# A fused SSD and attention layer on one core: the softmax division moved behind the value product, and the last norm part put into the issue table

## The chip, the cores and the metric

The kernel runs on one core of a Trainium2 chip. The time is device microseconds of one execution. Before the change three runs gave 640.44, 639.76 and 640.36 us, median 640.36.

## The reference

One layer of a streaming encoder, in fp32, for 512 tokens of a new stream ("prompt") and 64 tokens of a running one ("sample") with 256 cached frames. D = 1024. Cut to what the change touches:

```python
def mla_attend(...):
    s = einsum(q_lat, keys_c) + einsum(q_rope, keys_r)
    s = jnp.where(mask, s * scale, -jnp.inf)
    pr = jax.nn.softmax(s, axis=-1)          # the division by the row sum
    return einsum('bhqk,bkl->bqhl', pr, keys_c)
...
x = x + concat([y_ssd, o]) @ w_out
hf = rmsnorm(x, norm_ffn)
x = x + (silu(hf @ w_gate) * (hf @ w_up)) @ w_down
y = rmsnorm(x, norm_final)
```

There are eight attention heads of 64 value columns. The softmax divides each row of exponentials by its sum; the value product then sums over keys. The final norm divides every token by the root of its mean square over the 1024 channels. Beside this the layer has a chunked SSD (Mamba-2) branch with a causal convolution, whose output `y_ssd` is the other half of the input of `w_out`.

## The kernel before

Activations lie with channels on the 128 partitions and the 576 tokens (512 + 64) along the free axis. Most fp32 products are made of three fp32r products: each operand is split into a high part (ACT cast, L127/L157/L719) and a low part (DVE subtract, L128/L159/L720), so an evacuation of a product that feeds another product costs one ACT and one DVE instruction.

The stages by the trace: first projections and convolution until about 90 us, the SSD until about 150, attention with the output product until about 235, the gate/up and down products (Strassen-like block products, L894, L1034) until about 601, and last the final down tiles with the final norm (L1132 to L1262) until the end.

Attention works on pairs of heads `p` = 0..3. For a pair and a block of 128 query tokens `i` = 0..3, `scores` (L680) makes one PSUM bank `sc` per head, up to 512 keys wide; `soft` (L656 to L671) takes the row maximum on DVE (`mx`, L663), the exponential on ACT with the row sum accumulated (`pr`, `sm`, L664), the reciprocal of both sums on DVE (L665), and divides: head 0 by a DVE multiplication (L670), head 1 by an ACT scaling (L668). `turn` (L702, L704) transposes the divided blocks on PE into banks `ptp` of the tag "pp" and copies them to SBUF as `pt`, head 0 by ACT, head 1 by DVE. `values` (L727) sums V times `pt` into a bank `pv`, also of tag "pp", 64 partitions per head and 512 tokens wide; `cat` (L719, L720) splits `pv` into high and low parts `cat_o`. `out_tile` multiplies with `w_out` (banks `ps_o`); its first half takes `cat_y` (the SSD output), its second half `cat_o` of the four pairs. The sample tokens (`i` = 4, banks `sc_s`, `ptp_s`, `pvs`) go the same way with 64 tokens.

The last stage computes the eight channel tiles of y in two column parts of 320 and 256 tokens. For part 1 (256 columns) each tile t has 12 matmuls into `ps_l1_t` (L1104), a DVE addition to the residual `x2[t]` (L1145), an ACT square (`sq`, L1233) and, for t < 7, an ACT scaling with the gain (L1149). Squares of tiles 0 to 3 are summed by POOL, and ones-matmuls (`packed`, L1203) sum over channels. Ln and Exp on ACT and three DVE instructions make the norm factor (L186 to L193), eight small matmuls spread it over the partitions (`ps_r`, L1257), ACT copies one of the two spread banks to SBUF (`R`, L1258), and the tiles are multiplied by it: t = 0 and 1 on POOL from `R` (L1157), the others on DVE from PSUM (L1159, L1155), then stored.

Inside each engine the order of instructions is not left to a scheduler: a table of ranges per engine (`ISSUE`) lists the program's instructions in the order in which the engine issues them, and a second table (`PLACES`) says which buffer slot each tile gets. SP issues nearly all weight loads in one such order. Only the last part of the final norm stood outside of the table, in a block with a manual schedule (L1210 onward), in program order.

Of the kernel before, what the change touches and what calls it, by code (L numbers as in the profile page):

```python
# [19 lines left out]
P = 128  # L20
# [17 lines left out]
BLOCKS = tuple(range(0, LAST - 1, 4))  # L38
SEEDED = (4, 5, 6, 7)
# [17 lines left out]
def hybrid_layer_kernel(ctx: ExitStack, tc: tile.TileContext, a, o):  # L57
# [596 lines left out]
    prs, pts = {}, {}  # L654

    def soft(p, i, scs, nk):  # L656

        n = len(scs)
        mx = ap_.tile([P, 2], F32, tag="mx", name="mx", bufs=4)
        sm = ap_.tile([P, 2], F32, tag="sm", name="sm", bufs=4)  # L660
# [4 lines left out]
        dve.reciprocal(sm[:, :n], sm[:, :n])  # L665
        for j in range(n):
            if j:
                act.activation(pr[:, j], pr[:, j], AF.Identity, scale=sm[:, j : j + 1])  # L668
            else:
                dve.tensor_scalar(pr[:, j], pr[:, j], sm[:, j : j + 1], None, ALU.mult)  # L670
        prs[p, i] = pr  # L671

# [49 lines left out]
    def values(p):  # L722
        pv = bank("pp", f"pv{p}")
        for b in range(4):
            for j in range(2):
                h = 2 * p + j
                pe.matmul(  # L727
                    pv[64 * j : 64 * j + 64, b * P :], V[b][:, h * HD : (h + 1) * HD], pts[p, b, j],
                    start=b == 0, stop=True, skip_group_check=b > 0,
                )  # L730
        cat(p, pv, slice(0, TP))
# [464 lines left out]

    W1 = parts[1].stop - parts[1].start
# [11 lines left out]
    with tc.manual_schedule(engines={pe.engine, dve.engine, pool.engine, act.engine}):  # L1209
        pn0, pn1 = lbank("sc", "ps_n3_0", 0), bank("pp", "ps_n3_1")  # L1210
        first, second, _ = norm_steps(pn0, pn0, D, eps=False)
        q = []
        sent = [set(), set()]

        def out(i, k, r, rp):
            t = ORDERS[i][k]
            outs(i, t, r, rp)
            sent[i].add(t)
            if i == 0 and t ^ 1 in sent[i]:
                send(i, t & 6, 2, sp)  # L1220

        for t in range(KT):
            p = lbank(("hm", "sc", "pp")[t % 3], f"ps_l1_{t}", 1)
            down_half(p, last_terms(t), parts[1])
            if t == 2:
                pe.matmul(pn0, ones, ss3[:, parts[0]], start=True, stop=True)
                first()
            add(t, 1, p)
            if t == 2:
                second()  # L1230
                act.copy(R3[:, parts[0]], pn0)
            q.append(tmp("sq", W1))
            act.activation(q[t], x2[t][:, parts[1]], AF.Square)  # L1233
            if t < KT - 1:
                gain(t, 1)

            for k in {0: (), 1: (1, 0)}.get(t, (t,) if t < NP else ()):
                pool.tensor_tensor(ss3[:, parts[1]], ss3[:, parts[1]], q[k], ALU.add)  # L1238
            for k in OUTS.get(t, ()):
                out(0, k, pn0, R3[:, parts[0]])  # L1240
        packed(pn1, ss3[:, parts[1]], True, False)
        for t in range(NP, KT):
            packed(pn1, q[t], False, t == KT - 1)
        Rp = tmp("Rp", W2)
        first, second, _ = norm_steps(Rp, pn1[:, :W2], D, eps=False)
        first()
        second()

        warm = bank("hm", "ps_warm_last")
        for _ in range(7):  # L1250
            pe.matmul(warm[:, :P], ones, ones, start=True, stop=True)

        pr1 = [lbank("sc", f"ps_r3_{z}", 1) for z in range(2)]
        for z in pr1:
            for hf in range(2):
                row = ident[:, 64 * hf : 64 * hf + 1].to_broadcast([P, P])
                pe.matmul(z[:, hf * W2 : (hf + 1) * W2], row, Rp, start=True, stop=True)  # L1257
        act.copy(R3[:, parts[1]], pr1[1])  # L1258
        for k in range(KT):
            out(1, k, pr1[0], R3[:, parts[1]])  # L1260
        for t, q in SENDS:
            send(1, t, 1, q)  # L1262
# [25 lines left out]
0651423651426340315406516235041350264531645302406124531260546312045123450612345014652051342603541350124365310462054260  # L1288
534132025104623562453163052412365401546210503421602541356041536510223405632140562056143241564032
# [12 lines left out]
021021202120120120120120120120120102102012102102102102121021021201201201201201210210210202102102021  # L1302
# [3 lines left out]
0120210  # L1306
# [12 lines left out]
142-147 152-171 174 270-271 175-177 272-274 178-187 172-173 188-269 275-370 373-420 371 421-468 372 469-601 613-636  # L1319
602-612 637 641-644 638-640 657-659 665-688 660 689-736 661-662 737-760 771-794 663-664 645-652 763-766 653-656  # L1320
795-818 767-770 761-762 819-826 859-861 833-836 862-864 827-832 865-866 837-839 867 880-883 840 868-870 841 845-852
871-873 853-856 874-879 842-843 904-906 857-858 884-887 907-909 844 888 910-912 892-903 889-891 913-915 925-934
916-921 935 939-940 922-924 936-938 949-957 964-965 941 966 945-948 967-969 942-944 970-971 958-963 972-974 976-979
975 987-988 980 984-985 1003 991-993 981-983 986 1015 1004-1006 989 994-995 1016-1021 996 1007-1014 1022-1026
1029-1034 997 1043-1045 990 1000-1002 998-999 1046-1054 1035-1042 1027-1028 1059-1060 1055 1075-1092 1056-1058
1093-1104 1121-1123 1065-1067 1124 1061-1062 1071-1072 1063-1064 1130-1132 1068-1070 1125-1129 1073 1133-1156
1105-1108 1074 1229-1237 1119-1120 1238 1241 1239-1240 1242-1252 1157 1111-1114 1109-1110 1253-1264 1158 1176
1265-1276 1115-1118 1159-1161 1177-1179 1162-1175 1277-1285 1289-1290 1180-1183 1188-1189 1184-1187 1205-1206
1190-1192 1227 1193-1198 1291-1297 1199-1201 1228 1202-1204 1286-1288 1215-1220 1207-1214 1221 1318 1222-1224 1298
1225-1226 1299-1306 1319 1307 1320 1308-1317 1321-1322 1330-1332 1323 1342-1343 1348-1351 1344-1345 1352-1354 1346  # L1330
1355 1347 1333 1324-1329 1334-1341 1356-1363 1368 1364-1366 1369-1370 1367 1371-1393 1404 1394-1396 1405-1406
1397-1403 1407-1415 1428 1416-1427 1429-1433 1440-1441 1434-1435 1442 1436-1439 1572 1443-1447 1452 1448 1453-1456
1449 1457-1458 1450 1459-1460 1451 1461-1462 1587 1578 1584 1463 1581 1573 1464-1478 1579 1479-1486 1575 1488 1487
1489 1585 1490-1497 1500 1498 1501-1503 1499 1586 1588 1504-1506 1576 1574 1507 1580 1508-1509 1512 1577 1513 1510
1514-1515 1511 1516-1517 1605 1518-1522 1593 1523-1525 1582-1583 1526-1527 1606 1528-1531 1602 1536 1532 1537 1533
1538 1534 1603 1539 1607 1535 1589 1540-1541 1599 1542-1544 1594 1608 1545-1550 1600 1551-1552 1595 1614 1553-1555
1609 1560 1556-1557 1626 1561-1565 1615 1558-1559 1566-1568 1616 1569-1570 1604 1571 1596 1590 1597-1598 1601 1591
1610 1617 1620 1623 1621 1635 1627 1622 1592 1636 1629 1637 1628 1611 1641 1618 1630 1624 1631 1612-1613 1625
1658-1659 1642 1644 1650 1660 1647 1661-1662 1632-1633 1663 1651 1648 1664-1665 1619 1656 1638-1640 1666 1643 1667
1634 1668 1645 1669 1646 1649 1652-1654 1657 1694 1670-1672 1695-1697 1673 1682 1698 1655 1674 1699 1675 1700 1718  # L1340
1683 1719 1676-1677 1701 1678 1684 1702 1679 1685 1703 1680 1704 1686 1681 1720 1687 1721 1688 1722-1723 1689 1724
1690-1691 1706 1692-1693 1725 1707 1726 1705 1727-1728 1708-1709 1730 1710-1711 1729 1712 1731-1732 1713-1717
1733-1734 1778-1779 1735 1780 1754 1736 1755 1742 1756 1743-1744 1781 1737 1782 1745-1746 1766 1747-1749 1767 1783
1750-1752 1738 1768 1753 1757-1758 1769 1739-1740 1759 1741 1770 1784 1760 1785-1786 1771 1787 1761-1762 1802 1788
1803 1772 1789 1763 1773 1804-1805 1774 1806-1813 1764-1765 1775-1776 1838 1777 1839-1841 1862-1864 1842 1865
# [267 lines left out]
```

## Time and profile before

| what | value |
|---|---|
| median of three runs | 640.36 us |
| the profiled execution's own time | 639.58 us |
| its span (first to last instruction) | 637.5 us |
| around the span | 2.08 us |
| PE busy | 626.2 us, 98% |
| DVE busy | 551.4 us, 86% |
| ACT busy | 390.4 us, 61% |
| POOL busy | 70.7 us, 11% |
| mean granted PE clock | 0.998 |

PE is TensorE's matmul row, PEld its weight loads, DVE VectorE, ACT ScalarE, POOL GpSimd, SP SyncE (which issues DMAs). In a timeline a row is: start, busy time, engine, line, operation, tiles out<-in, shape, count; in brackets the idle time of the engine ahead of it and what ended that. In the table of windows each engine has its busy time in the stretch.

### The profile page before, as it was taken

The numbers are of one execution on the slowest core, as the hardware profiler recorded it, in microseconds if no ns is written. First come the engines' busy times: TensorE is split into PE (matmuls) and PEld (weight loads), VectorE is DVE, ScalarE is ACT, GpSimd is POOL, SyncE is SP. The second block draws the span as 40 slices with busy tenths as digits, with TensorE's granted clock in tenths as the row PEclk, the third lists the DMA queues.
The fourth block names the chain that finished last, engine by engine and source line by source line (L and its number), as shares of the span: only waits on it lengthen the run. The fifth ranks groups of instructions, "written<-read, shape, count | busy, mean of one in ns | idle before, by whom it ended". The sixth has DMA issues, their size and how long they took to land.

```text
span 637.5 us, 11950 instructions
## 1 busy us (share of the span) xinstructions
PE 626.2 (98%) x4639; PEld 598.0 (94%) x4639; DVE 551.4 (86%) x980; ACT 390.4 (61%) x751; POOL 70.7 (11%) x111
## 2 busy tenths in 40 slices
PE   9999999999999999999999999999999999999994
PEld 9899999985887899999999999999999999999994
DVE  6999996899867599999998997889888998998763
ACT  7655425789766479955656565655565656545463
POOL 1322122001010000000012002100211011100022
PEclk9999999999999999999999999999999999999999
DMA  9522185314131132231187427550765274723004
GB/s 310 207 51 78 35 209 151 114 30 147 72 111 34 62 131 73 93 108 67 36 202 158 128 91 163 141 136 40 189 159 133 67 182 111 181 74 133 1 1 149
DMA packets 31560, 72.66 MB, mean 114 GB/s; under 512 B 3706, under 2 KB 11400, under 8 KB 31248
## 3 DMA queue, kind: packets, MB, share of 16 engines
q1 hardware_dynamic: 25360, 60.77, 29.8%
q0 software_dynamic: 5424, 10.57, 9.3%
q8 instruction: 36, 0.59, 0.4%
q10 hardware_dynamic: 720, 0.57, 0.3%
q14 instruction: 20, 0.16, 0.1%
HBM read 58.03 MB, written 3.30 MB: 96 GB/s over the span
## 4 chain that ended last, share of the span: by engine, by line
PE 48%; issue 1%; DVE 1%; ACT 1%; POOL 1%; POOLq 0%; DVEq 0%
PE ps_x L894 17%; PE ps_dx L1034 9%; PE ps_z L894 9%; PE ps_dz L1034 5%; PE ps_y L894 4%; PE ps_dy L1034 2%; PE ps_l L1104 2%; POOL x L1157 0%; DVE x L1145 0%; DVE sq_last L1194 0%; DVE ss L1192 0%; POOL ss L1238 0%; POOLq L1600 0%; ACT sq L1233 0%; ACT x L1149 0%
## 5 line engine op out<-in xcount | busy, mean ns | idle before, releaser
L894 PE MATMUL ps_x<-xop,wh_gu_S 128*128 128x288 f32 x504 | 126.2, 295 | 0.0
L894 PEld LDWEIGHTS ps_x<-xop,wh_gu_S 128*128 128x128 f32 x504 | 88.2, 188 | 0.7 <-ACT u L963 0.2
L894 PE MATMUL ps_x<-xop,wl_gu_S 128*128 128x288 f32 x252 | 73.2, 295 | 0.0
L894 PE MATMUL ps_z<-xop,gu_a 128*128 128x288 f32 x252 | 61.7, 295 | 0.0
L127 ACT CAST wh_gu_S<-gu 128x1024 fp32r<-128x1024 f32 x44 | 46.2, 1053 | 14.8 <-PE ps_y L894 4.2
L128 DVE TENSOR_TENSOR wl_gu_S<-gu,wh_gu_S 128x1024 fp32r<-128x1024 f32 x44 | 52.8, 1217 | 0.8 <-ACT wh_gu_S L127 0.5
L894 PEld LDWEIGHTS ps_x<-xop,wl_gu_S 128*128 128x128 f32 x252 | 47.1, 188 | 0.0
L1047 POOL DMA_DIRECT2D x<-db x16 | 14.9, 930 | 277.9 <-ACT db L1040 247.8
L143 PE MATMUL ps_in<-xs,wh_in 128*128 128x288 f32 x256 | 45.5, 298 | 0.0
L894 PE MATMUL ps_y<-xop,wh_gu_A 128*128 128x288 f32 x168 | 44.9, 295 | 0.0
L894 PEld LDWEIGHTS ps_z<-xop,gu_a 128*128 128x128 f32 x252 | 43.5, 188 | 0.0
L894 PE MATMUL ps_z<-xop,wh_gu_S 128*128 128x288 f32 x168 | 43.4, 295 | 0.0
L894 PE MATMUL ps_x<-xop,wh_gu_A 128*128 128x288 f32 x168 | 42.7, 295 | 0.0
L143 PEld LDWEIGHTS ps_in<-xs,wh_in 128*128 128x128 f32 x256 | 37.8, 189 | 0.2
L127 ACT CAST wh_gu_A<-gu 128x1024 fp32r<-128x1024 f32 x22 | 23.1, 1051 | 23.0 <-PE ps_x L894 16.1
L894 PEld LDWEIGHTS ps_y<-xop,wh_gu_A 128*128 128x128 f32 x168 | 30.1, 188 | 0.1
L894 PEld LDWEIGHTS ps_z<-xop,wh_gu_S 128*128 128x128 f32 x168 | 29.7, 188 | 0.0
L128 DVE TENSOR_TENSOR wl_gu_A<-gu,wh_gu_A 128x1024 fp32r<-128x1024 f32 x22 | 26.8, 1217 | 3.3 <-ACT wh_gu_A L127 1.8
L894 PEld LDWEIGHTS ps_x<-xop,wh_gu_A 128*128 128x128 f32 x168 | 29.5, 188 | 0.0
L465 PE MATMUL ps_o<-cat_y,wh_out 128*128 128x288 f32 x128 | 29.0, 312 | 0.0
L143 PE MATMUL ps_in<-xs,wl_in 128*128 128x288 f32 x128 | 27.5, 296 | 0.0
L465 PE MATMUL ps_o<-cat_o,wh_out 128*128 128x288 f32 x128 | 27.3, 297 | 0.0
(594 smaller groups left out, 2002.8 us busy)
## 6 DMA issues: line engine op xcount, KB each, us to landing
gu<-in_w_gu SPq DMA_DIRECT2D x44, 512.0 KB, 4.8
db<-in_w_down SPq DMA_DIRECT2D x16, 512.0 KB, 4.5
x<-db POOLq DMA_DIRECT2D x16, 288.0 KB, 6.5
x<-dc POOLq DMA_DIRECT2D x16, 288.0 KB, 4.1
wr_in<-in_w_in SPq DMA_DIRECT2D x8, 512.0 KB, 6.2
wr_out<-in_w_out SPq DMA_DIRECT2D x8, 512.0 KB, 3.3
cumb<-cumD SPq DMA_DIRECT2D x5, 512.0 KB, 5.0
x<-in_xT SPq DMA_DIRECT2D x2, 1152.0 KB, 6.6
```

The costliest lines, as they stand in the source:

```text
L127: act.copy(hi, raw)
L128: dve.tensor_tensor(lo, raw, hi.bitcast(F32), ALU.subtract)
L143: pe.matmul(ps[:m, hf, :n], w, x[:, hf * n : (hf + 1) * n], start=start and k == 0 and i == 0, stop=stop and k == last and i == 2,)
L465: pe.matmul(ps[:, :n], w, x[:, cols], start=not onto and k == 0 and i == 0, stop=onto or (k == len(terms) - 1 and i == 2), skip_group_chec ...
L894: pe.matmul(ps, p, q, start=not onto and first and kp == kps[0] and j == 0, stop=onto or (last and kp == kps[-1] and j == 2), skip_group_c ...
L1034: pe.matmul(ps, l, r, start=not onto and k == 0 and j == 0, stop=onto or (k == n - 1 and j == 2), skip_group_check=onto,)
L1047: pool.dma_start(x2[t], v, accum_op=ALU.add)
L1104: pe.matmul(ps, w, x[:, cols], start=first and k == 0 and i == 0, stop=last and k == len(terms) - 1 and i == 2,)
```

## The change

It has two parts, and with them a new issue table and new slot numbers for both stages.

1. Softmax. For the prompt blocks `i` = 0..3 of all four pairs (`LATE_NORM`), `soft` stops after the exponential; the sums of a pair's four blocks and two heads are collected in one tile `sums` of 128 x 8. After the fourth block, `factor_rows` takes their reciprocal (DVE, 128x8), stores it transposed to DRAM (`rows`, 1024 elements of 4 bytes), and two DMAs read it back as rows broadcast over 64 partitions each (`rw`, 128 x 512). `values` multiplies `pv` by `rw` into an SBUF tile `pvn` (DVE), and `cat` splits that. The sample block keeps its division.
2. The end. The last stage's instructions are ordered by the table. Tile 7 of part 1 is seeded: ACT copies the residual into its PSUM bank, the products accumulate on it, its square is taken from PSUM and its last multiplication reads PSUM with `R`. The warm-up matmuls take another operand.

```diff
+LATE_NORM = (0, 1, 2, 3)
...
     def soft(p, i, scs, nk):
         n = len(scs)
+        late = i < 4 and p in LATE_NORM
...
+            sm = sums[p][:, 2 * i : 2 * i + 2]
...
+        if late:
+            prs[p, i] = pr
+            if all((p, k) in prs for k in range(4)):
+                factor_rows(p)
+            return
         dve.reciprocal(sm[:, :n], sm[:, :n])
...
+    def factor_rows(p):
+        dve.reciprocal(sums[p], sums[p])
+        rows = dpool.tile([8, P], F32, name=f"rows{p}")
+        sp.dma_start(rows.rearrange("k q -> q k"), sums[p])
+        rw[p] = tmp(f"rw{p}", TP)
+        for j in range(2):
+            src = rows.rearrange("(i j) q -> i j q", j=2)[:, j]
+            sp.dma_start(
+                rw[p][64 * j : 64 * j + 64].rearrange("p (i q) -> p i q", i=4), src.unsqueeze(0).to_broadcast([64, 4, P]),
+            )
...
     def values(p):
...
+        if p in LATE_NORM:
+            v = tmp(f"pvn{p}", TP)
+            dve.tensor_tensor(v, pv, rw[p], ALU.mult)
+            pv = v
         cat(p, pv, slice(0, TP))
...
-    def down_half(ps, terms, cols, first=True, last=True):
+    def down_half(ps, terms, cols, first=True, last=True, onto=False):
...
-                    ps, w, x[:, cols], start=first and k == 0 and i == 0, stop=last and k == len(terms) - 1 and i == 2,
+                    ps, w, x[:, cols], start=first and not onto and k == 0 and i == 0,
+                    stop=onto or (last and k == len(terms) - 1 and i == 2), skip_group_check=onto,
...
         if t == KT - 1:
-            dve.scalar_tensor_tensor(y, y, col(C_NL + t), r, ALU.mult, ALU.mult)
+            last = (y, r) if i == 0 else (seeded7[0], rp)
+            dve.scalar_tensor_tensor(y, last[0], col(C_NL + t), last[1], ALU.mult, ALU.mult)
...
-    with tc.manual_schedule(engines={pe.engine, dve.engine, pool.engine, act.engine}):
...
+        seeded = t == KT - 1
+        p = lbank("pp" if seeded else ("hm", "sc", "pp")[t % 3], f"ps_l1_{t}", 1)
+        if seeded:
+            seeded7.append(p)
+            act.copy(p, x2[t][:, parts[1]])
+        down_half(p, last_terms(t), parts[1], onto=seeded)
...
+        if not seeded:
             add(t, 1, p)
...
-            act.activation(q[t], x2[t][:, parts[1]], AF.Square)
+        act.activation(q[t], p if seeded else x2[t][:, parts[1]], AF.Square)
...
-            pe.matmul(warm[:, :P], ones, ones, start=True, stop=True)
+            pe.matmul(warm[:, :P], ones, q[-1][:, :P], start=True, stop=True)
...
     "PE": """
-142-147 152-171 174 270-271 175-177 272-274 178-187 172-173 188-269 275-370 373-420 371 421-468 372 469-601 613-636
+142-147 152-171 174 270-271 175-177 272-274 178-187 172-173 188-269 275-370 373-420 371 421-468 372 469-601 613-615
```

Three places show the new order. The first is DVE while the last two pairs are finished; `pvn_2533` and `pvn_2748` are the products of pairs 2 and 3, `sums_2446` the sums of pair 3, `wl_out` the low half of a weight tile for the second half of the output product. Before (`cat_o_2567` and `cat_o_2766` are pairs 2 and 3):

```order
L665 RECIPROCAL sm<-sm 128x2
L720 TENSOR_TENSOR cat_o_2567<-pvs_2570,cat_o_2567 128x64
L670 TENSOR_SCALAR pr_4_2553<-pr_4_2553,sm 128x320
L670 TENSOR_SCALAR pr_1_2596<-pr_1_2596,sm 128x256
L720 TENSOR_TENSOR cat_o_2567<-pv_2558,cat_o_2567 128x512
```

And now, from the reciprocal of pair 3's sums past the product of pair 2 (pair 3's own product `pvn_2748` stands nine rows behind the last one shown):

```order
L686 RECIPROCAL sums_2446<-sums_2446 128x8
L785 TENSOR_TENSOR x_1_2043<-ps_o_7_0_2642,x_1_2043 128x288
L727 COPY pt_2_2503<-ptp_2_1_2509 128x384
L743 TENSOR_TENSOR cat_o_2535<-pvs_2538,cat_o_2535 128x64
L756 TENSOR_TENSOR pvn_2533<-pv_2524,rw_2408 128x512
L727 COPY pt_2_2547<-ptp_2_1_2553 128x384
```

The divisions of blocks 0 to 3 are gone; a product that needs the DMA-made tile `rw` stands among the copies that PE's value product waits for.

The second place is SP's queue of DMAs at the same time. Before:

```order
L134 DMA wr_out_4_2604<-in_w_out 128x1024
L783 DMA x_1_2055<-in_xT 128x2304
L134 DMA wr_out_7_2666<-in_w_out 128x1024
L134 DMA wr_out_0_2791<-in_w_out 128x1024
L134 DMA wr_out_2_2903<-in_w_out 128x1024
```

And now:

```order
L688 DMA rows_2406<-sums_2197 128x8x1
L135 DMA wr_out_0_2763<-in_w_out 128x1024
L692 DMA rw_2408<-rows_2406 64x4x128
L135 DMA wr_out_2_2875<-in_w_out 128x1024
L692 DMA rw_2408<-rows_2406 64x4x128
L688 DMA rows_2569<-sums_2446 128x8x1
L692 DMA rw_2571<-rows_2569 64x4x128 x2
```

The two weight loads of the second half of the output product stand behind the store of pair 2's rows, and pair 2's second read-back stands behind both.

The third place is ACT at the end, from the last squares to the copy of the spread factor. Before:

```order
L1233 ACTIVATE sq<-x_1_2055 128x256
L186 ACTIVATE nr_y<-ps_n_1_7502 128x128
L188 ACTIVATE nr_y<-nr_y 128x128
L189 ACTIVATE nr_u<-nr_y 128x128
L1258 COPY R_99<-ps_r_1_7694 128x256
```

And now:

```order
L1267 ACTIVATE sq<-x_1_2043 128x256 x3
L1267 ACTIVATE sq<-ps_l_7_7619 128x256
L1177 ACTIVATE x_1_2043<-x_1_2043,par 128x256
L187 ACTIVATE nr_y<-ps_n_1_7472 128x128
L189 ACTIVATE nr_y<-nr_y 128x128
L190 ACTIVATE nr_u<-nr_y 128x128
L1177 ACTIVATE x_0_2041<-x_0_2041,par 128x256 x3
L1177 ACTIVATE x_1_2043<-x_1_2043,par 128x256 x2
L1292 COPY R_99<-ps_r_1_7664 128x256
```

Five of the gain scalings moved from between the squares to behind the norm factor, ahead of the copy of `R`. On PE the seven warm-up matmuls moved from ahead of the `ps_r` matmuls to behind them, and the matmuls of tiles 4 to 7 of part 1 are interleaved instead of tile after tile.

More of the change, by code (lines that the diff above doesn't have):

```diff
@@ L1207, in done @@
             yield lambda: outs(i, t, r, rp)
-    with tc.manual_schedule(engines={pe.engine, dve.engine, pool.engine, act.engine}):
[L1210 to L1227, printed above, removed]
-            add(t, 1, p)
[L1229 to L1262, printed above, removed]
@@ new lines, in hybrid_layer_kernel, with out @@
+    pn0, pn1 = lbank("sc", "ps_n3_0", 0), bank("pp", "ps_n3_1")
+    first, second, _ = norm_steps(pn0, pn0, D, eps=False)
+    q = []
+    sent = [set(), set()]
+    def out(i, k, r, rp):
+        t = ORDERS[i][k]
+        outs(i, t, r, rp)
+        sent[i].add(t)
+        if i == 0 and t ^ 1 in sent[i]:
+            send(i, t & 6, 2, sp)
+    for t in range(KT):
+        seeded = t == KT - 1
[4 more added lines that the diff above has]
+        down_half(p, last_terms(t), parts[1], onto=seeded)
+        if t == 2:
+            pe.matmul(pn0, ones, ss3[:, parts[0]], start=True, stop=True)
+            first()
+        if not seeded:
+            add(t, 1, p)
+        if t == 2:
+            second()
+            act.copy(R3[:, parts[0]], pn0)
+        q.append(tmp("sq", W1))
+        act.activation(q[t], p if seeded else x2[t][:, parts[1]], AF.Square)
+        if t < KT - 1:
+            gain(t, 1)
+        for k in {0: (), 1: (1, 0)}.get(t, (t,) if t < NP else ()):
+            pool.tensor_tensor(ss3[:, parts[1]], ss3[:, parts[1]], q[k], ALU.add)
+        for k in OUTS.get(t, ()):
+            out(0, k, pn0, R3[:, parts[0]])
@@ new lines, in hybrid_layer_kernel @@
+    packed(pn1, ss3[:, parts[1]], True, False)
+    for t in range(NP, KT):
+        packed(pn1, q[t], False, t == KT - 1)
+    Rp = tmp("Rp", W2)
+    first, second, _ = norm_steps(Rp, pn1[:, :W2], D, eps=False)
+    first()
+    second()
+    warm = bank("hm", "ps_warm_last")
+    for _ in range(7):
+        pe.matmul(warm[:, :P], ones, q[-1][:, :P], start=True, stop=True)
+    pr1 = [lbank("sc", f"ps_r3_{z}", 1) for z in range(2)]
+    for z in pr1:
+        for hf in range(2):
+            row = ident[:, 64 * hf : 64 * hf + 1].to_broadcast([P, P])
+            pe.matmul(z[:, hf * W2 : (hf + 1) * W2], row, Rp, start=True, stop=True)
@@ L1263, in hybrid_layer_kernel @@
+    act.copy(R3[:, parts[1]], pr1[1])
+    for k in range(KT):
+        out(1, k, pr1[0], R3[:, parts[1]])
+    for t, q in SENDS:
+        send(1, t, 1, q)
     close(psH_)
@@ L1323 @@
[L1323 to L1327, printed above, removed]
```

381 lines of the change are left out of this document (201 added, 180 removed), and 3 rows, old and new, of the table ISSUE.

## The prediction

> **What bounds the kernel now.** I read the busy times first, then PE's waits, then the stretches, then single timelines. These are the waits of PE (waited for, total us, times, longest) that touch the change:
>
> ```profile
> span 637.5 us, 11950 instructions
> PE ptp L702 <- DVE pr L670: 0.9, 1, 0.9
> PE ps_n L1203 <- ACT sq L1233: 0.8, 2, 0.4
> PE ptp_s L710 <- DVE pr L670: 0.2, 1, 0.2
> ```
>
> PE is busy 98% of the span, and the recorded waits on the softmax division are 1.1 us in all, two events. The second view shows where: four stretches of 16 us, with the busy time of PE, PEld, DVE, ACT, POOL, then the clock, the DMA share and GB/s.
>
> ```profile
> 144.00:160.00 16.00, 14.75 (x76) 9.54 (x76) 15.77 (x41) 15.23 (x44) 1.96 (x4) 1.00 0.45 146
> 160.00:176.00 16.00, 16.00 (x108) 12.60 (x107) 12.75 (x28) 11.92 (x31) 0.00 (x0) 1.00 0.23 90
> 192.00:208.00 16.00, 16.00 (x112) 12.45 (x111) 11.54 (x31) 10.89 (x34) 0.00 (x0) 1.00 0.10 34
> 208.00:224.00 16.00, 16.00 (x137) 12.97 (x136) 9.17 (x23) 7.18 (x18) 0.00 (x0) 1.00 0.24 80
> ```
>
> Only from 144 to 160 does PE lose time (1.25 us), and there DVE is busy 15.77 of 16 us and ACT 15.23. Later PE is full and DVE and ACT have a third of their time free. So of attention only its first 10 us can gain much from lighter DVE and ACT; from 160 on removed work frees engines that have room. PE's own work is the same before and after (the same matmuls in another order), so the time moves only by waits.
>
> **Softmax, what goes.** The groups of divisions over the whole program (duration in ns min/median/max):
>
> ```profile
> L665 DVE RECIPROCAL sm<-sm x20: 140/154/169, 149.9 to 211.4; 128x2 f32<-128x2 f32 x16, 128x1 f32<-128x1 f32 x4
> L670 DVE TENSOR_SCALAR pr<-pr,sm x20: 264/378/481, 150.3 to 212.3; 128x512 f32<-128x512 f32 x4, 128x256 f32<-128x256 f32 x4, 128x384 f32<-128x384 f32 x4, 128x128 f32<-128x128 f32 x4
> L668 ACT ACTIVATE pr<-pr,sm x16: 391/562/732, 155.1 to 211.7; 128x256 f32<-128x256 f32 x4, 128x128 f32<-128x128 f32 x4, 128x512 f32<-128x512 f32 x4, 128x384 f32<-128x384 f32 x4
> ```
>
> Sixteen of each go: on DVE 16 x 0.154 + 16 x 0.378 = 8.5 us, on ACT 16 x 0.562 = 9.0 us, spread over 60 us. In the tight stretch that is some four or five of each, 2 to 3 us per engine, twice what PE loses there. PE's waits in it:
>
> ```profile
> 154.10 1.12 PE L680 MATMUL sc<-ks,qs 100*128 100x512 f32 x2
> 156.14 0.66 PE L702 MATMUL ptp<-ident,pr 128*128 128x128 f32 x4 [0.92 <-DVE pr L670]
> 159.27 0.41 PE L710 MATMUL ptp_s<-ident,pr 128*64 128x128 f32 x2 [0.21 <-DVE pr L670]
> ```
>
> The transposes that waited 0.92 us for a DVE division now need only the exponential, and DVE reaches the maxima ahead of it earlier. I take both waits as gone, **-1.13 us**. What is late next is the exponential on ACT itself, which loses the scalings. The bounds: 0, if ACT or DVE is as late by another instruction, and -2.5, if PE's modelled busy time hides as much again.
>
> **Softmax, what comes.** Per pair one small reciprocal, three DMAs on SP, and one DVE product of 128x512. No product of that kind stands in the profile; the nearest are the splits of the same bank:
>
> ```profile
> L719 ACT CAST cat_o<-pv x4: 577/585/589, 175.4 to 219.7; 128x512 fp32r<-128x512 f32 x4
> L720 DVE TENSOR_TENSOR cat_o<-pv,cat_o x4: 670/686/692, 179.3 to 221.2; 128x512 fp32r<-128x512 f32 x4
> ```
>
> So four times 0.69 us, 2.7 on DVE against 8.5 saved. Where it counts is that bank `pv` is free only after this product, whereas before it was free after both splits; behind it on DVE stand the `pt` copies for which PE's value products wait, and the next pair's transposes wait for the bank. In the new order PE has about 1 us of its own matmuls between the last value matmul of pairs 0, 1 and 2 and the first that needs the bank. Against 0.69 us plus whatever DVE still has ahead of it, I take 0.05 us each; the bounds are 0 and 0.7 each. For pair 3 the chain is product 0.69, cast 0.59, subtract 0.69, about 2.0 us, against this stretch of PE:
>
> ```profile
> 210.15 2.33 PE L727 MATMUL pv<-pt,V 128*64 128x512 f32 x16
> ...
> 219.33 0.33 PE L738 MATMUL pvs<-pts,V 128*64 128x64 f32 x4
> ...
> 221.69 0.42 PE L465 MATMUL ps_o<-cat_o,wh_out 128*128 128x288 f32 x2
> ```
>
> The first matmul on `cat_o` starts 2.0 us after the value products end (219.66), so the longer chain just fits; bounds 0 and 0.7. All four together I take as **+0.2 us** (0 to 2.8).
>
> **The round trip through DRAM** must be over when the product comes up. No transfer of 4-byte pieces is in the trace. The nearest issues (KB, median us from issue to landing):
>
> ```profile
> ecp<-cumD SPq DMA_DIRECT2D x10, 128.0 KB, 5.1
> wr_pair<-in_w_pair SPq DMA_DIRECT2D x4, 192.0 KB, 3.9
> wr_uv<-in_w_uv SPq DMA_DIRECT2D x1, 256.0 KB, 2.6
> wr_out<-in_w_out SPq DMA_DIRECT2D x8, 512.0 KB, 3.3
> out_convT<-nconv SPq DMA_DIRECT2D x1, 24.0 KB, 7.2
> cumD<-cumT POOLq DMA_DIRECT2D x1, 20.0 KB, 2.3
> ```
>
> The store costs 2.3 (a small store to DRAM) to 7.2 us (a small store in short pieces); I take 3.0, near the first, since it holds 4 KB and the queues are nearly idle from 192 on (share 0.10). The read-back is of the shape of `ecp`: 2.6 to 5.1, I take 3.9, plus 0.6 for the issue of the second half (my estimate). Sum **7.5 us**, from 5.5 to 12.9. The time there is:
>
> ```profile
> 201.28 1.22 DVE L128 TENSOR_TENSOR wl_out<-wr_out,wh_out 128x1024 fp32r<-128x1024 f32 x1
> ...
> 209.80 0.45 DVE L758 TENSOR_TENSOR x<-ps_o,x 128x288 f32<-128x288 f32 x1
> ```
>
> In the new order pair 3's reciprocal stands just ahead of the addition that was at 209.80, and its product can't start before the value products end at 219.66: 9.9 us. Pair 2's stands ahead of the `wl_out` that was at 201.28, and its values end at 210.15 + 2.33 = 212.48: 11.2 us. Pairs 0 and 1 have about 20. So the middle value hides entirely behind PE's own matmuls, with 2.4 us to spare, cost 0. Pair 2's second half stands behind a 512 KB weight load (3.3 us alone), which takes most of its spare time. SP's queue: the two `wr_out` loads now stand behind pair 2's store, but their splits come some ten us later against 3.3 us to land: 0.
>
> The Trainium skill speaks against small pieces: "DMA: Bandwidth & Descriptors", section Specifications, has transfers below 512 bytes done as read-modify-write, which none of these rows isolates; in "Anatomy of one DMA" it gives about 2.0 us fixed, and by that figure a store and a read-back in turn would take an estimated 4 us or more. Neither changes the sum above.
>
> **The end.** The rows that set it before:
>
> ```profile
> 625.96 0.51 ACT L1149 ACTIVATE x<-x,par 128x256 f32<-128x256 f32 x1
> 625.98 0.44 PE L1203 MATMUL ps_n<-sq,ones 128*64 128x128 f32 x4 [0.43 <-ACT sq L1233]
> 626.82 0.44 PE L1203 MATMUL ps_n<-sq,ones 128*64 128x128 f32 x4 [0.41 <-ACT sq L1233]
> 627.19 1.83 PE L1251 MATMUL ps_warm_last<-ones 128*128 128x128 f32 x14
> 627.31 0.28 ACT L186 ACTIVATE nr_y<-ps_n 128x128 f32<-128x128 f32 x1 [0.54 <-PE ps_n L1203]
> 629.03 1.16 PE L1257 MATMUL ps_r<-Rp,ident 128*128 128x128 f32 x8
> 630.23 0.37 ACT L1258 COPY R<-ps_r 128x256 f32<-128x256 f32 x1 [1.90 <-PE ps_r L1257]
> 630.68 1.41 POOL L1157 TENSOR_TENSOR x<-x,R 128x256 f32<-128x256 f32 x2 [5.62 <-ACT R L1258]
> ```
>
> The new order takes tile 7's addition (0.41) and the scalings from between the squares, and its square comes straight from PSUM. The last down matmul ended at 624.74; square 0.40, four ones-matmuls, and the 12 others flow meanwhile: Ln starts at about 626.24 rather than 627.31, **1.07 us** earlier, and so does `ps_r` (627.96). But five scalings now stand between the norm factor and the copy of `R`: from about 627.3 on, five times 0.47 (0.51 overlapping a little) makes 629.65, while the bank is ready at 629.16. So `R` starts at 629.67 instead of 630.23, and POOL, whose two products and drain end the kernel, is **0.56 us** earlier. I count **-0.55**; bounds -1.07 (the scalings fit in gaps) and +0.3 (the seed or the first part's norm makes PE wait).
>
> **Sum.** -1.13 + 0.2 + 0 - 0.55 = -1.48 us. On the profiled execution's own time, 639.58, that is 638.1; on the median of the runs, 640.36, which lies 0.78 higher and by which the result is told, **638.9 us**.
>
> **Rivals.** *The round trip is late* (the other side). With the chain at 12.9 us pair 3's product comes 3.0 us late and pair 2's 1.7; DVE issues in order, so `pt` copies and additions stand behind it, and PE has nothing else: 640.36 - 1.48 + 4.7 = 643.6. It loses all gain when the chain passes 11.3 us (0.1 + 1.4 late). For it: short-piece stores took 7.2, `ecp` 5.1, and weight loads share SP's queue. Against: those two ran at busy times. 0.20, with 641 to 644.
>
> *Attention gains nothing*: ACT at 15.23 of 16 us, or the wait for `pv`, takes the place of the division. Only the end is left: 640.36 - 0.55 + 0.2 = 640.0. For it: ACT is nearly as full as DVE. Against: ACT sheds 2 us there. 0.18.
>
> *PE is slow at the end*: the warm-up matmuls no longer fill the 1.8 us ahead of `ps_r`. At the start of the program the cold rows read:
>
> ```profile
> 1.07 3.78 PE L218 MATMUL ps_warm<-ones 128*128 128x128 f32 x16 [1.07 <-POOL nepsb L110]
> ```
>
> That is 0.24 us per matmul against 1.83 / 14 = 0.13: the eight `ps_r` would take up to 0.9 us more, and the end gains nothing: 639.8. The Trainium skill, "TensorE: Matmul & The Clock Gate", Part 1, lets the clock fall only after an idle window of about 3.4 us; by that rule the 1.8 us here would not suffice, and no run yet shows it. 0.07.
>
> *More is hidden in PE's rows*: attention gives 2.5 to 3 instead of 1.13: 637.1. 0.10.
>
> **How the numbers follow.** The forecast has 0.45, its own range 638.0 to 639.8. The range to hold 8 in 10 takes in the hidden gain and most of the late round trip: 636.7 to 642.2. A measurement of this kernel tells about 0.2% (1.28 us) from no change: faster means below 639.08. Of the forecast's 0.45 some 0.32 lie below, with the hidden gain and a tenth of the rest 0.48; slower is the late round trip beyond 641.6 and a pair of small waits, 0.20; the same 0.32.
>
> **What would show it.** Right: in the changed profile the stretch at 144 to 160 has PE above 15.5 us; no wait of DVE on `rw` and no PE wait on `pvn` above 0.3; Ln of the last norm 1.5 us after the last down matmul, and `R` held up by scalings. Wrong: an idle DVE ahead of `pvn` ended by a DMA (then the time is that idle time more), PE waiting for `ptp` on ACT's exponential as long as before, or a `ps_r` group above 1.5 us.

## The result and the profile after

The change makes the kernel slower: 654.93 us median (654.64 to 656.46, 5 runs) against 639.76 (639.42 to 640.44, 5 runs) before, ratio 1.0237 with a 95% interval of 1.0225 to 1.0249. That is 15.2 us more; the prediction was 638.9 us, range 636.7 to 642.2. The profiled execution took 654.93 us, its span 652.9.

The head of the page of the changed kernel:

```profile
span 652.9 us, 11935 instructions
PE 633.2 (97%) x4639; PEld 603.4 (92%) x4639; DVE 550.0 (84%) x955; ACT 382.5 (59%) x736; POOL 71.0 (11%) x111
...
PE 88%; DMA 6%; ACT 2%; DVE 2%; issue 1%; SPq 0%; POOL 0%; DVEq 0%; ACTq 0%; POOLq 0%
```

The span grew by 15.4 us. PE has the same 4639 records as before but is busy 633.2 us instead of 626.2, 7.0 us longer, and idle 19.7 instead of 11.3, 8.4 us more: so half of the loss is waiting and half is the same work done more slowly. In the chain that ended last (third line) transfers hold 6%. The chain of the kernel before can't be set beside it, since it could be followed back only over half of its span, to the gate/up products.

PE's longest waits, then what DVE and ACT waited for when they kept PE waiting (waited for, total us, times, longest):

```profile
PE ptp L725 <- DVE pvn L756: 6.9, 1, 6.9
PE sc L703 <- ACT pr L671: 3.0, 2, 2.8
PE ps_r L1291 <- DVE Rp L194: 1.8, 1, 1.8
```

```profile
DVE pvn L756 <- DMA rw<-rows: 8.9, 1, 8.9
```

```profile
ACT pr L671 <- DMA rows<-sums: 4.6, 1, 4.6
```

The waits for the division, 0.9 and 0.2 us before, are gone. In their place PE waits 6.9 us for a value bank, because the product with the factor rows on DVE waits 8.9 us for the read-back; and 2.8 us for an exponential that ACT could not write, because its row sums go to a slot that pair 0's store had not yet released.

The stretches of the attention stage (busy us of PE, PEld, DVE, ACT, POOL; then the clock, DMA share, GB/s):

```profile
144.00:160.00 16.00, 15.28 (x71) 10.22 (x70) 14.05 (x30) 13.70 (x38) 1.96 (x4) 0.89 0.40 145
176.00:192.00 16.00, 13.21 (x78) 10.70 (x77) 6.72 (x16) 8.62 (x23) 1.57 (x4) 0.89 0.52 149
208.00:224.00 16.00, 12.10 (x96) 9.38 (x94) 5.66 (x15) 6.37 (x18) 0.00 (x0) 0.99 0.53 79
224.00:256.00 32.00, 27.99 (x201) 25.92 (x202) 24.79 (x42) 15.30 (x25) 0.00 (x0) 0.90 0.32 107
```

From 144 to 160, DVE fell from 15.77 to 14.05 us and PE's lost time from 1.25 to 0.72. That looks like the forecast gain, but PE's 15.28 us hold 71 matmul records where they held 76: part of them ran at half clock. The granted clock, 1.00 in the stretches of attention before, is now 0.89 to 0.90 in three of them. By slices of 1 us it reads 0.50 from 155.5 to 158.9, from 179.4 to 182.8, from 223.8 to 230.6 and, at the end, from 643.6 to 647.0: twice right behind a wait (2.8 and 1.8 us), once with the wait of 6.9 us still running, and once at 155 behind one of 0.34 us. PE was busy for 13.8 us of that time, which at full clock would be 6.9 us: about what its rows grew by (7.0).

SP's queue shows the round trip of pairs 1 and 2, and in the last line the store of pair 3 (start, us, issues):

```profile
191.08 0.38 SPq L688 DMA_DIRECT2D rows<-sums  x1
201.06 1.25 SPq L692 DMA_DIRECT2D rw<-rows  x2
204.47 0.38 SPq L688 DMA_DIRECT2D rows<-sums  x1
204.95 0.53 SPq L135 DMA_DIRECT2D wr_out<-in_w_out  x1
215.54 0.59 SPq L692 DMA_DIRECT2D rw<-rows  x1
216.22 0.55 SPq L135 DMA_DIRECT2D wr_out<-in_w_out  x1
216.82 0.58 SPq L692 DMA_DIRECT2D rw<-rows  x1
217.46 0.60 SPq L688 DMA_DIRECT2D rows<-sums  x1
```

Each read-back starts when its store has landed: 10.0 us after the issue for pair 1, 11.1 for pair 2. Pair 2's second half, issued at 216.82, lands 9.3 us later, at 226.15, and the weight load ahead of it, issued at 216.22, after 9.7. Both were issued after pair 2's store had landed, and just ahead of pair 3's store, which lands at 226.95. From store to rows that is 21.7 us for a product that could have started at 219.0, when its value products ended; PE stood still from 220.1. The issues by kind (KB, median us to landing) between 160 and 232, the changed kernel first, then the one before:

```profile
wr_out<-in_w_out SPq DMA_DIRECT2D x4, 512.0 KB, 8.0
x<-in_xT SPq DMA_DIRECT2D x1, 1152.0 KB, 15.2
rw<-rows SPq DMA_DIRECT2D x8, 128.0 KB, 4.3
qs<-rrp POOLq DMA_DIRECT2D x4, 36.0 KB, 6.3
rows<-sums SPq DMA_DIRECT2D x4, 4.0 KB, 10.0
```

```profile
wr_out<-in_w_out SPq DMA_DIRECT2D x6, 512.0 KB, 3.3
x<-in_xT SPq DMA_DIRECT2D x1, 1152.0 KB, 7.5
qs<-rrp POOLq DMA_DIRECT2D x4, 36.0 KB, 2.2
```

A store of 4 KB takes 10 us, and what else moves at that time takes two to three times as long as before, weight tiles on SP's queue and the rotated part of q (`qs<-rrp`) on POOL's too. Of the four weight loads the one that was issued between two stores, at 188.26, landed after 3.3 us as before; the other three took 6.3, 9.7 and 12.2. The store itself hardly occupies the DMA engines. While pair 1's was alone in flight (10 us, columns as above), their share was 0.05:

```profile
191.00:201.00 10.00, 10.00 (x76) 9.78 (x76) 5.62 (x14) 4.59 (x13) 0.00 (x0) 1.00 0.05 2
```

Where the 15.4 us of span lie, by three marks read from the timelines of PE:

| mark | before | after | later by |
|---|---|---|---|
| first score matmul of attention | 145.88 | 145.97 | 0.09 |
| first gate/up matmul `ps_x` | 259.20 | 276.02 | 16.82 |
| last down matmul `ps_l` ends | 624.74 | 640.51 | 15.77 |
| end of the span | 637.54 | 652.89 | 15.35 |

Attention loses 16.7 us; the gate/up and down products between the second and the third mark gain 1.05, and the end, from the last down matmul on, 0.42.

### The profile page after: what moved, and what is told of

The parts are those of the page before. It is cut to its first block, busy times and chain, and to the rows that moved or that the text cites. A ratio compares the mean times of both kernels' runs of the same rounds, so it can differ in the third digit from the quotient of the medians.

```text
span 652.9 us, 11935 instructions
## 1 busy us (share of the span) xinstructions
PE 633.2 (97%) x4639; PEld 603.4 (92%) x4639; DVE 550.0 (84%) x955; ACT 382.5 (59%) x736; POOL 71.0 (11%) x111
## 4 chain that ended last, share of the span: by engine, by line
PE 88%; DMA 6%; ACT 2%; DVE 2%; issue 1%; SPq 0%; POOL 0%; DVEq 0%; ACTq 0%; POOLq 0%
PE ps_x L921 21%; PE ps_z L921 10%; PE ps_dx L1061 9%; PE ps_in L144 8%; PE ps_o L466 6%; PE ps_y L921 5%; PE ps_dz L1061 4%; PE ps_z L466 4%; PE ps_l L1131 4%; DMA rows<-sums 3%; PE ps_first L144 2%; PE ps_dy L1061 2%; PE ps_p L921 2%; DMA rw<-rows 1%; PE sc L703 1%; DMA gu<-in_w_gu 1%
## 5 line engine op out<-in xcount | busy, mean ns | idle before, releaser
L466 PE MATMUL ps_o<-cat_y,wh_out 128*128 128x288 f32 x128 | 35.3, 343 | 1.0 <-DVE x L785 1.0
L703 PE MATMUL sc<-ks,qs 100*128 100x512 f32 (+3 forms) x64 | 24.6, 478 | 3.0 <-ACT pr L671 3.0
```

What stands on the lines that cost most here:

```text
L466: pe.matmul(ps[:, :n], w, x[:, cols], start=not onto and k == 0 and i == 0, stop=onto or (k == len(terms) - 1 and i == 2), skip_group_chec ...
L703: pe.matmul(s[:, :nk], qs[:, j, q0 : q0 + P], ks[:, j, :nk], start=True, stop=True)
```

## The experiments

Theory A stood first: the store is slow, and those pay who wait for it directly. Theory B: the new order and the longer hold of the value bank cost the time. Each comparison is with the kernel before on the same chip.

**Four slots for the sums (e1_sums4).**

```diff
-sums[p] = ap_.tile([P, 8], F32, tag="sums", name=f"sums{p}", bufs=2)
+sums[p] = ap_.tile([P, 8], F32, tag="sums", name=f"sums{p}", bufs=4)
```

> Four slots instead of two for the tile of the row sums, so that pair 2's exponentials no longer wait until pair 0's store has read the slot. Theory A (the store of 4-byte pieces is slow, about 10 us, and whatever waits for it pays, first through the slot, then through the factor rows, each time followed by some 3.4 us of PE at half clock): the wait of 2.8 us at 178 and the half clock behind it go, 1.7 us more, so about 650.4 us; the wait of 6.9 us for pair 2's factor rows stays. Theory B (the new order and the longer hold of the value bank cost the time, the DMA waits only show where): the wait moves to another instruction, 654 us or more.

Measured 658.43 us, ratio 1.0275 (1.0254 to 1.0295): slower than the change itself. The slot wait is gone, but two products wait for their rows now (one before):

```profile
PE ptp L725 <- DVE pvn L756: 11.4, 2, 8.4
```

So a wait that is taken away ahead of a store comes back behind it. Theory A's 650.4 is missed; theory B's mark, 654 or more with the wait moved, is met, although the waits are still ended by transfers.

**Factor rows that don't depend on the store (e2_rwfree), and both edits (e3_both).**

```diff
-src = rows.rearrange("(i j) q -> i j q", j=2)[:, j]
+src = a["ident"][:8].rearrange("(i j) q -> i j q", j=2)[:, j]
```

> The factor rows are read from an input in DRAM of the same shape instead of from the stored sums (so the values are not divided by their sums; the store is still made). All instructions and the order stay. Theory A: the 6.9 us wait of pair 2's product goes with the half clock behind it (about 1.8 us more), about 646 us; the slot wait of 2.8 us stays. Theory B: 652 us or more.

> Both edits: four slots for the sums and factor rows from an input (the values are not divided by their sums). Theory A: nothing waits for the store any more; both waits and the half clock behind them go, 13.2 us, about 641.5 us, and if the division's own saving of 1.1 us holds, 640 to 641. Theory B: 648 us or more.

Measured 655.57 us (ratio 1.0230, 1.0209 to 1.0250) and 657.71 (1.0255, 1.0238 to 1.0272). Theory A falls: in the kernel with both edits nothing needed the stored numbers any more, and the time stayed. Theory B's marks, 652 and 648 or more, are met again. The issues of the kernel with both edits:

```profile
rw<-in_ident SPq DMA_DIRECT2D x8, 128.0 KB, 15.4
rows<-sums SPq DMA_DIRECT2D x4, 4.0 KB, 11.9
```

The rows are issued 0.4 to 2.4 us behind the store, from an input, and land after 15.4 us (median), later than when they waited for the store. What counts is not the dependence on the store but being in flight with it. From this comes theory C: the store holds up the transfers behind it (and, as pair 2's second half showed, those issued just ahead of it).

**The store in pieces of 4, 8, 32 and 16 bytes for pairs 0 to 3, with four slots (e4_pieces).**

```diff
+w = (1, 2, 8, 4)[p]
-sp.dma_start(rows.rearrange("k q -> q k"), sums[p])
+sp.dma_start(
+    rows.rearrange("k q -> (k q)").rearrange("(a q b) -> q a b", b=w, q=P), sums[p].rearrange("q (a b) -> q a b", b=w),
+)
```

> Four slots for the sums, and the store of 1024 numbers cut into pieces of 4, 8, 32 and 16 bytes for pairs 0, 1, 2 and 3 (the factor rows come back permuted). Theory P (the number of pieces sets the store's time): 4 bytes 10 us, 8 bytes about 6, 16 bytes about 4, 32 bytes about 3. Theory Q (traffic on the queues, or the write to DRAM as such): all four near 10 us. Under P pair 2's product waits about 5 us less than with four slots alone.

A single run gave 647.74 us, 10.7 under the kernel with four slots alone. SP's queue, where a read-back again starts when its store has landed:

```profile
165.93 0.38 SPq L689 DMA_DIRECT2D rows<-sums  x1
...
178.08 1.25 SPq L695 DMA_DIRECT2D rw<-rows  x2
...
191.46 0.38 SPq L689 DMA_DIRECT2D rows<-sums  x1
195.87 1.25 SPq L695 DMA_DIRECT2D rw<-rows  x2
206.05 0.33 SPq L689 DMA_DIRECT2D rows<-sums  x1
...
207.46 0.58 SPq L695 DMA_DIRECT2D rw<-rows  x1
...
217.71 0.38 SPq L689 DMA_DIRECT2D rows<-sums  x1
221.25 1.25 SPq L695 DMA_DIRECT2D rw<-rows  x2
```

The same 4 KB take 12.1 us in pieces of 4 bytes, 4.4 in 8, 1.4 in 32 and 3.5 in 16 (pair 3). Theory P holds in direction, theory Q falls. Number and size of the pieces change together here, and each size stands for one pair with its own traffic beside it.

**32-byte pieces for all pairs, with four slots (e8_32b).**

```diff
-sp.dma_start(rows.rearrange("k q -> q k"), sums[p])
+sp.dma_start(rows.rearrange("k q -> (k q)").rearrange("(q k) -> q k", q=P), sums[p])
```

> Four slots for the sums, and the store of every pair's 1024 numbers in 128 pieces of 32 bytes instead of 1024 of 4 (the factor rows come back permuted, so the values are divided by the wrong sums). Theory C (the store of 4-byte pieces holds up all transfers behind it on the DMA engines for about 10 us: factor rows, weight tiles, the rotation of q): with short stores (1.4 us to land, as pair 2's 32-byte pieces took) nothing waits, the factor rows are there after about 6 us, and the attention part costs no more than before: 639 to 641. Theory B (the new order and the hold of the value bank cost a good part of it by themselves): 644 us or more, with PE waits that no transfer ends.

Measured 640.70 us, ratio 1.0005 (0.9992 to 1.0018).

```profile
rw<-rows SPq DMA_DIRECT2D x8, 128.0 KB, 4.1
rows<-sums SPq DMA_DIRECT2D x4, 4.0 KB, 1.4
```

No DVE product waits for its rows any more and PE's busy time is 627.8 us. Theory C holds and theory B as it was stated (644 or more) falls: with the short store, all but about 1 us of the net loss is gone.

**4-byte pieces with those of each partition together (e11_lines)**, otherwise as e3_both:

```diff
-rows = dpool.tile([8, P], F32, name=f"rows{p}")
-sp.dma_start(rows.rearrange("k q -> q k"), sums[p])
+wide = dpool.tile([16, P], F32, name=f"rows{p}")
+rows = wide[:8]
+sp.dma_start(wide.rearrange("k q -> (k q)").rearrange("(q k two) -> q k two", q=P, two=2)[:, :, 0], sums[p])
```

> As the run with four slots and factor rows from an input (657.7 us), but the 1024 pieces of 4 bytes go to every second word in the order of the partitions, so that the eight pieces of a partition stand together and no two DMA engines write into the same 32 bytes (the values are not divided by their sums). Theory N (the number of 4-byte pieces alone makes the store slow): it lands after 10 to 12 us again and the time stays near 657. Theory L (pieces of several engines that fall into the same piece of memory hold each other up): it lands after 2 us or so, and the time falls to 640 or 641.

Measured 640.89 us, ratio 1.0013 (0.9998 to 1.0027), against 657.71 with the same number of pieces in the transposed place.

```profile
rw<-in_ident SPq DMA_DIRECT2D x8, 128.0 KB, 8.7
rows<-sums SPq DMA_DIRECT2D x4, 4.0 KB, 6.9
```

Both theories have a part. The place is worth 5 us of the store (11.9 to 6.9) and 6.7 of the read-backs behind it; the number and size of the pieces keep it at 6.9, where 128 pieces take 1.4. The 5 us decide: pair 2's rows now land at 212.8, and its product starts at 214.5, when its value products are done. That pieces of several partitions side by side hold each other up is theory L's reading; the runs show what the place costs, not why.

**A quick store that computes the same (e12_16b).** The sums are ordered by head, stored in 256 pieces of 16 bytes and read back as they stand; the product reads them with a stride of four.

```diff
-sm = sums[p][:, 2 * i : 2 * i + 2]
+sm = sums[p].rearrange("q (j i) -> q i j", j=2)[:, i]
...
+rows = dpool.tile([2, TP * 4 // 4], F32, name=f"rows{p}")
+sp.dma_start(rows.rearrange("j (q i) -> q j i", i=4), sums[p].rearrange("q (j i) -> q j i", j=2))
...
+sp.dma_start(rw[p][64 * j : 64 * j + 64], rows[j : j + 1].to_broadcast([64, TP]))
...
+dve.tensor_tensor(
+    v.rearrange("p (i q) -> p i q", i=4), pv.rearrange("p (i q) -> p i q", i=4), rw[p].rearrange("p (q i) -> p i q", i=4), ALU.mult)
```

> The changed kernel with a quick store that computes the same: the sums ordered by head, stored in 256 pieces of 16 bytes, read back as they stand, and the product reads them with a stride; four slots for the sums. Theory C (only the store's length mattered): as with 32-byte pieces, 640 to 641, level with before. Rival: the strided read or the 16-byte pieces cost, 643 or more.

Measured 640.60 us, ratio 1.0006 (0.9992 to 1.0021). Theory C again: this is the change without its fault, level with before. The strided product took 1.08 us instead of 0.69. The stretches answer to those above:

```profile
144.00:160.00 16.00, 15.08 (x79) 10.32 (x79) 14.15 (x31) 13.71 (x38) 1.95 (x4) 1.00 0.40 145
176.00:192.00 16.00, 16.00 (x114) 14.31 (x113) 8.82 (x21) 10.10 (x28) 1.92 (x4) 1.00 0.22 62
208.00:224.00 16.00, 15.94 (x135) 12.63 (x134) 10.98 (x23) 7.53 (x20) 0.00 (x0) 1.00 0.15 41
224.00:256.00 32.00, 31.06 (x228) 30.08 (x227) 30.20 (x52) 25.31 (x45) 0.00 (x0) 1.00 0.36 122
```

PE is full again from 176 to 224, but for 0.06 us, and the clock is 1.00 throughout. Still PE loses 0.92 us at 144 to 160 and 0.94 at 224 to 256, where it lost 1.25 and nothing before.

**The end alone (e6_tail)**: the division and the order of before in attention, the change's last stage.

```diff
-LATE_NORM = (0, 1, 2, 3)
+LATE_NORM = ()
```

The tables are those of before up to the last stage and those of the change behind it.

> The end of the change alone: attention with the division on the probabilities and in the order of before, the last stage in the new order with the seeded tile. By the two traces (12.8 us from the last down matmul to the end before, 12.4 after) 0.4 us faster than before, ratio 0.9993. Rival: the 0.4 is lost, because the start of the last stage depends on what came ahead of it: 1.000.

Measured 637.75 us, ratio 0.9959 (0.9944 to 0.9973): faster than both kernels, and by more than expected. Its end, ACT's norm factor, the spreading matmuls, the copy and POOL:

```profile
625.23 0.28 ACT L187 ACTIVATE nr_y<-ps_n 128x128 f32<-128x128 f32 x1 [0.47 <-PE ps_n L1233]
...
626.15 2.09 ACT L1177 ACTIVATE x<-x,par 128x256 f32<-128x256 f32 x5
...
626.95 1.16 PE L1291 MATMUL ps_r<-Rp,ident 128*128 128x128 f32 x8 [1.77 <-DVE Rp L194]
...
628.15 0.37 ACT L1292 COPY R<-ps_r 128x256 f32<-128x256 f32 x1
...
628.59 1.41 POOL L1186 TENSOR_TENSOR x<-x,R 128x256 f32<-128x256 f32 x2 [5.50 <-ACT R L1292]
```

The last down matmul ends at 623.94, Ln starts 1.29 us later (2.57 before), the span ends 11.5 us later (12.8 before): 1.28 us gained, three times the 0.42 of the changed kernel. The ratio is worth some 2.6 us; where the rest lies the runs don't show (in this profile 0.71 us of it stand ahead of attention, where the two kernels are the same). In the changed kernel, at half clock, the same matmuls took 2.02 us and the copy waited for them:

```profile
643.52 2.02 PE L1291 MATMUL ps_r<-Rp,ident 128*128 128x128 f32 x8 [1.77 <-DVE Rp L194]
...
645.58 0.37 ACT L1292 COPY R<-ps_r 128x256 f32<-128x256 f32 x1 [0.77 <-PE ps_r L1291]
```

**The warm-up matmuls back ahead of the spreading matmuls, with the end alone (e7_tailwarm) and with 32-byte pieces (e10_32bwarm).** PE's table, last line:

```diff
-... 4358 4364-4380 4388-4391 4381-4387
+... 4358 4364-4391
```

> The end of the change alone, with the warm-up matmuls ahead of the spreading matmuls. Theory W: 0.7 to 0.9 us faster than with the changed place of the warm-up matmuls, 1.1 to 1.3 us faster than before, ratio 0.998. Rival (the scalings hold up the copy): as the run before, 0.9993.

> As the run before, with the seven warm-up matmuls of the last norm ahead of the matmuls that spread its factor, as they were before the change. Theory W (PE is at half clock there because it idles 1.8 us ahead of them): these eight take 1.2 us instead of 2.0 and the end is 0.7 to 0.9 us earlier than in the run before. Rival (the clock doesn't matter, since the scalings on ACT hold up the copy): the same within 0.2 us.

Measured 638.31 us, ratio 0.9971 (0.9959 to 0.9984), and 640.04, ratio 0.9999 (0.9987 to 1.0012): no gain over the runs without it, whose intervals overlap these. In all four profiles the spreading matmuls take 1.16 us, with and without the warm-up, and the span ends 11.5 us after the last down matmul. Theory W's condition isn't met: the clock did not fall at that place in any of the four, though PE idled 1.8 us in two of them. Whether the warm-up would keep it up where it does fall stays open.

**The old order with the quick 16-byte store: all pairs (e13_old_all), pair 0 alone (e14_old_p0).** Both have the new end; the four or one products and reciprocals are put into the old tables.

```diff
-LATE_NORM = ()
+LATE_NORM = (0, 1, 2, 3)   (e13_old_all)
+LATE_NORM = (0,)           (e14_old_p0)
```

> The order of before in attention with the new end, and the division of all four pairs moved behind the value product with the quick 16-byte store. Theory O (the new attention order costs the time that remains): the two waits of 1.1 us for the division go and nothing comes in their place, 1 us under the end alone (ratio to before 0.994). Rival M (the moved division itself costs it: the exponentials on ACT and the longer hold of the value bank take the place of the waits): as the end alone or slower, 0.996 to 1.000.

> The same for pair 0 alone, the pair whose division PE waited for. Theory O and a weaker M (only the later pairs' banks are held too long): the 1.1 us wait goes at the price of one product, ratio 0.994 to 0.995. Rival M: the transposes wait for ACT's exponentials just as long, 0.996 or more.

Measured 642.43 us, ratio 1.0024 (1.0014 to 1.0035), and 638.68, ratio 0.9967 (0.9955 to 0.9980). The end alone gave 0.9959, so pair 0's late division gains nothing and that of all pairs loses. PE's waits, with pair 0 alone, then with the end alone:

```profile
PE sc L700 <- ACT pr L671: 0.6, 2, 0.3
PE ptp_s L730 <- DVE pr L682: 0.6, 1, 0.6
```

```profile
PE ptp L725 <- DVE pr L682: 0.9, 1, 0.9
...
PE ptp_s L733 <- DVE pr L682: 0.2, 1, 0.2
```

The 0.9 us wait for the division is gone; 0.6 for the exponentials that free the score banks and 0.4 more for the sample block's division have taken its place, 1.2 against 1.1. Rival M holds for pair 0. For all pairs the old order was not tuned to the later products (1.9 us of waits for exponentials, 0.8 for a `pt` copy, 0.8 for `cat_o`), and the profile fell on its slowest run (644.72) and has 3.4 us of half clock at 195, so its size says little.

## Why the prediction was wrong

The direction, size and range were wrong, by one step above all: "So the middle value hides entirely behind PE's own matmuls, with 2.4 us to spare, cost 0." The round trip through DRAM did not hide, and its store held up other transfers with it; with a short store in its place (e12_16b) about 0.4 of the 15.2 us is left (ratio 1.0006). A premise failed beside it: "PE's own work is the same before and after [...], so the time moves only by waits"; 7.0 of the 15.4 us of span are the same rows done more slowly.

- **The store.** Taken at 3.0 us, bounded by 2.3 and 7.2; it took 9.5 to 11.7. The neighbours in the trace were chosen by size; the shortest pieces among them, those of `out_convT`, were 192 bytes (24 KB in 128). With 32-byte pieces the same 4 KB land in 1.4 us, with each partition's 4-byte pieces together in 6.9. The fixed 2.0 us that the prediction takes from the Trainium skill, "DMA: Bandwidth & Descriptors", section "Anatomy of one DMA", are given there for DMAs issued from GpSimd; this store stood on SP's queue.
- **The chain.** Taken at 7.5 us and at most 12.9; pair 2's took 21.7: 11.1 for the store, 1.3 until the second read-back was issued behind a weight load, and 9.3 for that read-back, with pair 3's store in flight beside it (6.1 and 5.4 with the short stores of e8_32b and e12_16b). The cover, estimated at 11.2 us, was even longer: PE's wait began at 220.1, 15.6 us after the store's issue.
- **Left out: what else moves beside the store.** The rows themselves when they need nothing from it (15.4 us to land), the weight tiles (8.0 against 3.3), the rotated part of q (6.3 against 2.2). I counted SP's queue as an order of issues only, and so priced the round trip for its own reader alone.
- **Left out: the two slots of `sums`.** Pair 2's exponentials waited 4.6 us until pair 0's store had released its slot. Taking that wait away gained nothing, since the next wait was behind it.
- **Left out: the clock.** 7.0 of the 15.4 us are PE's own rows at half clock behind and around the waits. With the quick store all but 1.3 of them go too (PE busy 627.5 us, 626.2 before).
- **The late round trip as rival** had the right mechanism and, with pair 2, the right place (pair 3's rows came in time), and was given 0.20 and 644 at the most. Its sign came, an idle DVE ahead of `pvn` ended by a DMA, but "that idle time more" would be 8.9 us, not 15.2.
- **Attention, -1.13 us.** The two waits for the division did go, but others came, as the rival with 0.18 had it. The change with the quick store is 1.0006 of before, the end alone 0.9959: its attention part still costs about 0.47%, 3 us. By the marks, first score matmul to first `ps_x` takes 115.4 us with 32-byte pieces and the warm-up in place and 116.4 with the quick store, 113.3 before. In the last two PE is busy for 114.1 and 112.1 us of it, with the same 789 records at full clock: 2.0 of these 3.1 us are longer rows and not waits. The gate/up and down products behind gain 1.1. What of these 2 to 3 us is the new order and what the hold of the value bank stays open; with pair 0 alone it was no gain, not a loss.
- **The end, -0.55 us.** Measured -0.42 in the changed kernel, but as the sum of 1.28 gained and 0.86 lost to half clock (2.02 against 1.16 us). I let the five scalings hold up the copy of `R`; they took 2.09 us, not 2.35, and in e6_tail they ended as the bank was ready, so the copy followed the matmuls at once. So the earlier norm factor, 1.28 us by the trace (1.07 forecast), passed through whole. The rival of the slow PE (0.07, up to 0.9 us) is what the changed kernel shows.

## What to carry to other kernels

Price a transfer by its pieces and where they land, not by its bytes, and then ask what moves beside it: four transposing stores of 4 KB cost 15 us of a 640 us kernel, and no less when nobody read what they had stored. If a small result must be turned on its way through memory, store it as it lies in longer pieces and let the reader turn it with a stride (16 bytes were enough here). And a wait on a full PE is paid more than once where the clock falls behind it, so count PE's busy time at equal work beside the waits.

## What the runs showed of the hardware

- 1024 words of 4 bytes took 9.1 to 12.1 us to store to DRAM when neighbouring words came from different partitions, 6.9 (median of four) when each partition's words stood together; 512 pieces of 8 bytes 4.4 (one store), 256 of 16 between 1.6 and 3.5, 128 of 32 bytes 1.4 (but for one of 3.0 and one of 3.6). The Trainium skill, "DMA: Bandwidth & Descriptors", section Specifications, has all transfers under 512 bytes done as read-modify-write; the trace agrees that small pieces are slow, but below that size they still differ eightfold (1.4 against 12.1 us).
- A slow store held up transfers of other queues as well: `qs<-rrp` on POOL's queue took 6.3 us beside it, 2.9 in the same order with 32-byte pieces and 2.2 before. It also held up transfers issued just ahead of it: 9.3 us for a read-back issued 0.6 us earlier. Alone in flight it kept the DMA engines busy for 5% of its time; what it spends the rest on no run shows.
- PE's clock read 0.50 for 3.4, 6.8 or 10.2 us at a time, and in each profile its changes lie whole multiples of 3.41 us apart (in the changed kernel it stayed up for 44, 6, 12 and 121 times that, in turn, before it fell). It fell after a wait of 2.8 us and within one of 6.9. With the changed place of the warm-up PE idled 1.8 us ahead of the spreading matmuls: in the changed kernel they took 2.02 us behind it, with factor rows from an input and four slots 1.83, with the four piece sizes 1.80, and in the other eight kernels with that order 1.16. At 155 us the clock fell behind a recorded wait of only 0.34, in the changed kernel and with 32-byte pieces, and not in the other seven profiles with that order. The Trainium skill, "TensorE: Matmul & The Clock Gate", Part 1, gives an idle window of about 3.4 us as the condition; these runs show falls after less. What decides stays open: behind the same 1.8 us ahead of the same matmuls the clock fell in three profiles of eleven.
